# Two-layer encoder on one core: a reworked opening, and one step moved ahead of a store in the tail

## The chip, the core and the metric

The kernel runs on one core of a Trainium2 chip. The core has five instruction queues: TensorE (PE in the profile; its weight loads are listed as PEld), VectorE (DVE), ScalarE (ACT), GpSimd (POOL) and SyncE (SP). SyncE here does nothing but issue transfers; ScalarE and GpSimd issue some too. Each queue runs in its own order, and an instruction waits for semaphores that other queues or transfers set. The metric is the device time of one execution in microseconds (us), lower is better.

## The reference

Input and output are 512 tokens by 1024 features in float32. Two layers run one after the other. Each normalizes x, projects it by a 1024 x 3072 matrix, runs eight heads of stick-breaking attention and four pairs of differential attention, projects back and adds to x; then comes a dense block with a squared ReLU. A last normalization ends it.

```python
for l in range(DEPTH):
    h = rmsnorm(x, attn_norm[l])
    proj = jnp.einsum('bsd,de->bse', h, w_in[l])
    ...
    x = x + jnp.einsum('bse,ed->bsd', mixed, w_o[l])
    h = rmsnorm(x, mlp_norm[l])
    u = jnp.square(jax.nn.relu(jnp.einsum('bsd,df->bsf', h, w_ff1[l])))
    x = x + jnp.einsum('bsf,fd->bsd', u, w_ff2[l])
return rmsnorm(x, final_norm)
```

`rmsnorm(x, g)` is x times the inverse root of the mean of its squares over the features, times g.

## The kernel before

**Layout.** x lies transposed in SBUF: eight chunks (numbered 0 to 7) of 128 features by 512 tokens. A float32 product is made of three TensorE products. Each operand is split into a rounded high part (`hi`) and the rest (`lo`), and hi*hi, hi*lo and lo*hi are added in PSUM. ScalarE makes the high part, VectorE the low part by a subtraction that needs the high part. So for every chunk of x and every block of weights there is a step on ScalarE, then one on VectorE, then products on TensorE.

**Opening.** The first layer's normalization factor is applied after the projection, so TensorE can begin as soon as the first chunk has landed and has been scaled by its gains (`make_h`, line 249). The first two weight units, `raws[0]` and `raws[1]` (called unit 0 and unit 1 here; tiles `whi0`, `wlo0`, `whi1`, `wlo1`), feed two PSUM banks `p00` and `p01`. Both need all eight chunks. Each unit has eight blocks of 128 columns, block c for chunk c. The tile `begin` holds the gains and block 0 of unit 0; it comes over ScalarE's transfer queue, and so do blocks 1 to 3 of unit 0. The chunks of x and the rest of both units come over SyncE's queue in the order of lines 205 to 209.

**Warm-up.** Eight products of zeros (lines 222 and 223) run on TensorE ahead of the data. They read the zero part of the tile `edge`, which GpSimd sets (line 217) behind the set-up of the identity matrix (line 214).

**Order.** A scheduler places the instructions of each queue, guided by the order of the code and by the pairs given to `behind(a, b)`, which puts a after b on one engine. The order is fixed at build time. Each transfer from SyncE or ScalarE takes the next of eight semaphores in turn, and the ninth waits until the first has landed, and so on.

**Tail.** The last product form ("22") of the last group finishes the output, one row of 128 tokens after another: rows 0, 1, 2 and 3, each in two halves of 512 features. For a row, `square` on ScalarE adds up the squares of both halves, `root` adds them on VectorE (line 1161) and takes the power -1/2 on GpSimd (line 1163), and `store` multiplies one half on VectorE and the other on ScalarE and issues the transfers. Row 3 goes through `last_row` and `store_last` in quarters. Two lists, `first` for VectorE and `squares` for ScalarE, are chained by `in_order` (line 1286), so their order is that of lines 1250 to 1255.

Of the kernel before, what the change touches and what calls it, by code (L numbers as in the profile page):

```python
# [9 lines left out]
F32 = mybir.dt.float32  # L10
F32R = mybir.dt.float32r
BF16 = mybir.dt.bfloat16
AF = mybir.ActivationFunctionType
# [4 lines left out]
P = 128  # L18
S = 512
# [146 lines left out]
def trunk(ctx, tc, opened, xT, w, w2, w1, gfin, lamv, cos, sin, out):  # L166
    nc = tc.nc
# [10 lines left out]
    def bank(tag, name):  # L178
        if tag == "any":
            tag = ("mm", "s", "s", "mm", "s")[turn[0] % 5]  # L180
            turn[0] += 1
        ring[0] += tag == "s"
        return ps.tile([P, 512], F32, tag=tag, name=name, bufs=banks[tag])
# [17 lines left out]
    lam_ex = cp.tile([P, L, 2], F32, tag="lamex", name="lam_ex")  # L201
    raws = [wraw.tile([P, 1024], F32, tag="raw", name=f"raw{i}") for i in range(2)]
    nc.scalar.dma_start(begin, opened)
    nc.scalar.dma_start(raws[0][:, P : 4 * P], w[0][:, P : 4 * P])
    for c in range(KC):
        nc.sync.dma_start(x[:, c, :], xT[c])
        if c % 2 == 0:
            for i in range(c < 4, 2):
                nc.sync.dma_start(raws[i][:, c * P : (c + 2) * P], w[i][:, c * P : (c + 2) * P])
    W.raw = dict(enumerate(raws))  # L210
    W.loaded = 2
    W.load(3)

    make_identity(nc, ident)
    mhalf = cp.tile([P, 4], F32, tag="mhalf", name="mhalf")
    nc.vector.memset(mhalf, -0.5)
    nc.gpsimd.memset(edge[:, 0:384], 0.0)
    prime = cp.tile([P, 1], F32, tag="prime", name="prime")
    nc.scalar.activation(prime, mhalf[:, 0:1], AF.Exp)
    zeros = edge.bitcast(BF16)  # L220
    pw = bank("t", "warm")
    for _ in range(WARM):
        nc.tensor.matmul(pw, zeros[:, 0:128], zeros[:, 128:640], start=True, stop=True)

    def gcol(which, l, c):
        i = {"attn": l * 8, "mlp": 16 + l * 8, "final": 32, "sub": 40 + l}[which] + c
# [19 lines left out]
            out=lo, in0=src, scalar=-1.0, in1=hi.bitcast(F32), op0=ALU.mult, op1=ALU.subtract)  # L246
        return a

    def make_h(c, g):
        a = nc.scalar.activation(h_hi[:, c, :], x[:, c, :], AF.Copy, scale=g)  # L250
        return a, nc.vector.scalar_tensor_tensor(
            out=h_lo[:, c, :], in0=x[:, c, :], scalar=g, in1=h_hi[:, c, :].bitcast(F32),
            op0=ALU.mult, op1=ALU.subtract)

    def add_sq(c, first, sqt, eng=nc.gpsimd):
# [80 lines left out]
    for l in range(L):  # L336
        with ExitStack() as actx:
# [22 lines left out]
            if l == 0:  # L360
                W.eager = True
                W.split_part(0, 0, P)
                W.eager = False
                opened = make_h(0, gcol("attn", 0, 0))
                behind(opened[1], W.last[1])
                W.split_part(1, 0, 2 * P)
                for a, b in zip(W.last, opened):
                    behind(a, b)
                ahead = W.last
                W.split_part(0, P, 2 * P)  # L370
                for a, b in zip(W.last, ahead):
                    behind(a, b)
                for c in range(1, KC):
                    if c % 2 == 0:
                        for i in range(2):
                            W.split_part(i, c * P, (c + 2) * P)
                            if (c, i) == (2, 0):
                                for a, b in zip(W.last, opened):
                                    behind(a, b)
                    opened = make_h(c, gcol("attn", 0, c))  # L380
                    if c == 1:
                        for a, b in zip(opened, W.last):
                            behind(a, b)
                W.split = 2
            else:
                pts, halfway, opened = opened_by.pop()
# [399 lines left out]
            def dense(pts):  # L786
                if l == 0:
                    us = [W.next("x"), W.next("x")]
                    pts = [bank("mm", f"p{l}{i}") for i in range(2)]
                    for i, m in ((0, 0), (0, 2), (1, 0), (0, 1), (1, 1), (1, 2)):  # L790
                        a, b = wpair(us[i], 0), hpair(0)
                        nc.tensor.matmul(pts[i], a[m == 2], b[m == 1], start=m == 0, stop=False)
                    yield 6 * 0.216
                    for i, m in ((0, 0), (1, 0), (0, 2), (1, 2), (0, 1), (1, 1)):
                        a, b = wpair(us[i], 1), hpair(1)
                        nc.tensor.matmul(pts[i], a[m == 2], b[m == 1], start=False, stop=False)
                    yield 6 * 0.216
                    turns = [(c, i) for c in range(2, 5) for i in range(2)] + [(c, i) for i in range(2) for c in (5, 6, 7)]
                    for c, i in turns:
                        three(pts[i], wpair(us[i], c), hpair(c), False, c == KC - 1)  # L800
                        yield 3 * 0.216
                step, b = 2 * KC, int(ORDER[0][1])
                held = [(pts[0], "d", b, "q"), (pts[1], "d", b, "k")]
                def walk(name, kind, b, which):
                    if kind in "wu":
                        for _ in all_values() if kind == "w" else values_of(b):
                            yield None
                    else:
# [50 lines left out]
        with ExitStack() as fctx:  # L859
# [331 lines left out]
            for g in range(GROUPS):  # L1191
# [24 lines left out]
                for form in FORMS2:  # L1216
# [20 lines left out]
                    for n, (c, i, r, part) in enumerate(work):  # L1237
# [11 lines left out]
                              opens and n == mine[0] and part < 2, n == mine[-1], not opens)  # L1249
                        if tail and last and n == 3:  # L1250
                            squares += [square(0, 0), seed, square(1, 0)]
                            first += [weighed[2], turned[1], came[1], root(0), weighed[3], store(0, 0, False)]
                            squares.append(store(0, 1, True))
                            first += [root(1), *gather(total, to, (0,)), store(1, 0, False)]
                            squares += [store(1, 1, True), square(2, 1)]
                        if end and not last and form == "22" and n % 2:
                            h = back(n // 2)
# [122 lines left out]
```

## Time and profile before

| What | us |
|---|---|
| median of 3 runs (lowest, highest) | 1124.26 (1123.91, 1124.55) |
| the profiled execution's own time | 1124.27 |
| its span, first to last instruction | 1122.5 |
| around the span in that execution | 1.77 |
| TensorE busy in the span | 1114.8 |
| VectorE, ScalarE, GpSimd busy | 903.4, 682.7, 153.6 |

In the timeline a row gives the start, the length, the engine (with a q for its instruction queue, where transfers are issued), the line, the operation, the tiles written and read, the shapes, and how many were merged; behind it in brackets stands how long the engine had been idle and what ended that. Matmuls overlap, so their rate is read from starts, not from lengths. The rows on transfers give the time from issue until the data had landed.

### The profile page before, as it was taken

Reading aid. Unit: us, or ns where it says so; the run is one execution under the profiler, and the core shown is the slowest. Engines: PE = TensorE matmul, PEld = TensorE weight load, DVE = VectorE, ACT = ScalarE, POOL = GpSimd, SP = SyncE. Lnnn points to the kernel's source line nnn. Section 1 sums busy time; section 2 is a strip of 40 time slices with the busy share of each in tenths; the row PEclk is TensorE's granted clock in tenths of the full one; section 3 lists DMA queues with packets and bytes.
Section 4 is the critical chain, followed back from the end, with each engine's and each line's share of the span. In section 5 each row is a group of like instructions: output and inputs, shape, how many; then the busy total and the mean of one; then the engine's idle time right before and its main releaser. Section 6 shows DMA issues by size and latency. Waiting matters only on the chain.

```text
span 1122.5 us, 17199 instructions
## 1 busy us (share of the span) xinstructions
PE 1114.8 (99%) x6377; PEld 978.2 (87%) x6377; DVE 903.4 (80%) x1309; ACT 682.7 (61%) x1107; POOL 153.6 (14%) x233
## 2 busy tenths in 40 slices
PE   9999999999999999999999999999999999999997
PEld 7889889888899899899878898988888998998986
DVE  7788788798668779779877887887787787797787
ACT  6446666667558457467344566665774584674665
POOL 1001344101011001001000014430011010010010
PEclk9999999999999999999999999999999999999999
DMA  7466343268687678658325654512676786787462
GB/s 249 137 191 184 112 133 114 73 220 232 172 217 169 182 200 185 189 134 211 109 75 148 197 146 130 168 59 76 209 175 183 202 189 175 184 185 206 113 132 94
DMA packets 61043, 181.25 MB, mean 161 GB/s; under 512 B 7456, under 2 KB 8736, under 8 KB 60960
## 3 DMA queue, kind: packets, MB, share of 16 engines
q1 hardware_dynamic: 50160, 141.84, 40.0%
q0 software_dynamic: 10368, 37.75, 19.2%
q8 instruction: 50, 0.82, 0.3%
q10 hardware_dynamic: 432, 0.56, 0.1%
q14 instruction: 33, 0.27, 0.1%
HBM read 150.77 MB, written 4.19 MB: 138 GB/s over the span
## 4 chain that ended last, share of the span: by engine, by line
PE 98%; DVE 1%; issue 0%; POOL 0%; ACT 0%; POOLq 0%; DVEq 0%
PE X L300 9%; PE X L302 9%; PE X L301 9%; PE V L300 4%; PE V L302 4%; PE V L301 4%; PE wo L300 3%; PE wo L301 3%; PE wo L302 3%; PE f L300 3%; PE f L302 3%; PE f L301 3%; PE Y L300 2%; PE Y L302 2%; PE Y L301 2%; PE W L302 1%
## 5 line engine op out<-in xcount | busy, mean ns | idle before, releaser
L117 ACT ACTIVATE whi<-q 128x1024 fp32r<-128x1024 f32 x96 | 101.7, 1059 | 108.5 <-PE X L302 38.1
L133 DVE TENSOR_TENSOR wlo<-q,whi 128x1024 fp32r<-128x1024 f32 x96 | 117.1, 1222 | 46.5 <-ACT whi L117 46.3
L133 DVE TENSOR_TENSOR wlo<-raw,whi 128x1024 fp32r<-128x1024 f32 (+1 forms) x82 | 97.2, 1191 | 11.0 <-ACT whi L117 11.0
L117 ACT ACTIVATE whi<-raw 128x1024 fp32r<-128x1024 f32 (+1 forms) x82 | 80.8, 993 | 37.6 <-issue 8.9
L300 PE MATMUL X<-whi,Ah 128*128 128x512 f32 x248 | 97.7, 394 | 0.0
L301 PE MATMUL X<-wlo,Ah 128*128 128x512 f32 x248 | 96.8, 390 | 0.0
L302 PE MATMUL X<-whi,Al 128*128 128x512 f32 x248 | 96.7, 390 | 0.0
L133 DVE TENSOR_TENSOR wlo<-waves,whi 128x1024 fp32r<-128x1024 f32 x40 | 48.9, 1221 | 16.5 <-ACT whi L117 16.4
L117 ACT ACTIVATE whi<-waves 128x1024 fp32r<-128x1024 f32 x40 | 42.2, 1055 | 29.7 <-PE X L302 20.5
L300 PEld LDWEIGHTS X<-whi,Ah 128*128 128x128 f32 x248 | 46.6, 188 | 12.0 <-DVE y L1104 1.9
L302 PEld LDWEIGHTS X<-whi,Al 128*128 128x128 f32 x248 | 46.6, 188 | 9.9
L302 PE MATMUL X<-hxh,wlo 128*128 128x256 f32 x192 | 54.4, 283 | 0.0
L302 PE MATMUL X<-h_hi,wlo 128*128 128x256 f32 x192 | 54.4, 283 | 0.0
L301 PE MATMUL X<-hxl,whi 128*128 128x256 f32 x192 | 54.4, 283 | 0.0
L301 PE MATMUL X<-h_lo,whi 128*128 128x256 f32 x192 | 54.4, 283 | 0.0
L300 PE MATMUL X<-hxh,whi 128*128 128x256 f32 x192 | 54.4, 283 | 0.0
L301 PEld LDWEIGHTS X<-wlo,Ah 128*128 128x128 f32 x248 | 46.6, 188 | 8.9
L300 PE MATMUL X<-h_hi,whi 128*128 128x256 f32 x192 | 54.4, 283 | 0.0
L300 PE MATMUL f<-h_hi,whi 128*128 128x512 f32 x128 | 50.4, 394 | 0.0
L302 PE MATMUL f<-h_hi,wlo 128*128 128x512 f32 x128 | 49.9, 390 | 0.0
L301 PE MATMUL f<-h_lo,whi 128*128 128x512 f32 x128 | 49.9, 389 | 0.0
L240 DVE TENSOR_TENSOR Al<-x,Ah 128x512 fp32r<-128x512 f32 (+1 forms) x60 | 46.5, 792 | 3.8 <-ACT Ah L239 3.5
(712 smaller groups left out, 3702.6 us busy)
## 6 DMA issues: line engine op xcount, KB each, us to landing
raw<-in_w SPq DMA_DIRECT2D x78, 512.0 KB, 3.6
q<-in_w SPq DMA_DIRECT2D x48, 512.0 KB, 4.6
q<-in_w POOLq DMA_DIRECT2D x48, 512.0 KB, 7.6
waves<-in_w SPq DMA_DIRECT2D x28, 512.0 KB, 4.5
first_a<-in_w SPq DMA_DIRECT2D x12, 512.0 KB, 4.7
first_b<-in_w SPq DMA_DIRECT2D x12, 512.0 KB, 5.2
first_c<-in_w SPq DMA_DIRECT2D x12, 512.0 KB, 4.3
first_b<-in_w POOLq DMA_DIRECT2D x12, 512.0 KB, 6.7
```

What stands on the lines that cost most here:

```text
L117: return self.nc.scalar.activation(o, src, AF.Copy)
L133: self.last = h, nc.vector.tensor_tensor(out=lo[:, a:b], in0=raw[:, a:b], in1=hi[:, a:b].bitcast(F32), op=ALU.subtract)
L240: nc.vector.tensor_tensor(out=lo, in0=src, in1=hi.bitcast(F32), op=ALU.subtract)
L300: nc.tensor.matmul(pt, ah, bh, start=first, stop=False, skip_group_check=goes_on),
L301: nc.tensor.matmul(pt, ah, bl, start=False, stop=False, skip_group_check=goes_on),
L302: nc.tensor.matmul(pt, al, bh, start=False, stop=last, skip_group_check=goes_on))
```

## The change

Opening:
- The warm-up products read a single zero (the low half of the float32 value -0.5 in the tile `mhalf`), broadcast over both operands, so they wait for VectorE's small write of `mhalf` and no longer for GpSimd's `edge`.
- Chunk 0 of x is loaded in two halves of 256 tokens, scaled in halves, and its first two products with unit 0 (high by high, high by low) are issued in halves too.
- Block 0 of unit 1 is loaded alone over ScalarE's queue, between `begin` and blocks 1 to 3 of unit 0; on SyncE's queue only block 1 of that unit is left at that place. The splits of blocks 0 and 1 are made one block at a time in a given order.

Tail: `root(1)`, the second row's sum and power, is put ahead of VectorE's store of the first row.

```diff
     nc.scalar.dma_start(begin, opened)
+    nc.scalar.dma_start(raws[1][:, 0:P], w[1][:, 0:P])
     nc.scalar.dma_start(raws[0][:, P : 4 * P], w[0][:, P : 4 * P])
     for c in range(KC):
-        nc.sync.dma_start(x[:, c, :], xT[c])
+        for t in ([slice(0, 256), slice(256, S)] if c == 0 else [slice(0, S)]):
+            nc.sync.dma_start(x[:, c, t], xT[c][:, t])
         if c % 2 == 0:
             for i in range(c < 4, 2):
-                nc.sync.dma_start(raws[i][:, c * P : (c + 2) * P], w[i][:, c * P : (c + 2) * P])
+                a = max(c, 1) * P
+                nc.sync.dma_start(raws[i][:, a : (c + 2) * P], w[i][:, a : (c + 2) * P])
...
-    make_identity(nc, ident)
     mhalf = cp.tile([P, 4], F32, tag="mhalf", name="mhalf")
     nc.vector.memset(mhalf, -0.5)
+    make_identity(nc, ident)
     nc.gpsimd.memset(edge[:, 0:384], 0.0)
...
+    nought = mhalf.bitcast(BF16)[:, 0:1]
     for _ in range(WARM):
-        nc.tensor.matmul(pw, zeros[:, 0:128], zeros[:, 128:640], start=True, stop=True)
+        nc.tensor.matmul(pw, nought.to_broadcast([P, P]), nought.to_broadcast([P, S]), start=True, stop=True)
...
-                opened = make_h(0, gcol("attn", 0, 0))
-                behind(opened[1], W.last[1])
-                W.split_part(1, 0, 2 * P)
-                for a, b in zip(W.last, opened):
-                    behind(a, b)
-                ahead = W.last
-                W.split_part(0, P, 2 * P)
-                for a, b in zip(W.last, ahead):
-                    behind(a, b)
+                halves = [slice(0, 256), slice(256, S)]
+                for t in halves:
+                    ahead, opened = W.last, make_h(0, gcol("attn", 0, 0), t)
+                    behind(opened[1], ahead[1])
+                    W.last = opened
+                for i, c in ((1, 0), (0, 1), (1, 1)):
+                    ahead = W.last
+                    W.split_part(i, c * P, c * P + P)
+                    for a, b in zip(W.last, ahead):
+                        behind(a, b)
...
-                        nc.tensor.matmul(pts[i], a[m == 2], b[m == 1], start=m == 0, stop=False)
+                        for t in halves if (i, m) in ((0, 0), (0, 2)) else [slice(0, S)]:
+                            nc.tensor.matmul(pts[i][:, t], a[m == 2], b[m == 1][:, t], start=m == 0 and not t.start, stop=False)
...
-                            first += [weighed[2], turned[1], came[1], root(0), weighed[3], store(0, 0, False)]
+                            first += [weighed[2], turned[1], came[1], root(0), weighed[3], root(1), store(0, 0, False)]
                             squares.append(store(0, 1, True))
-                            first += [root(1), *gather(total, to, (0,)), store(1, 0, False)]
+                            first += [*gather(total, to, (0,)), store(1, 0, False)]
```

On ScalarE, this is the order of the opening before, from the scaling of chunk 0 on (`h_hi` is a scaled chunk's high part, `whi0` and `whi1` are those of units 0 and 1; the fourth and sixth rows are chunks 1 and 2, the eighth is chunks 3 and 4):

```order
L250 ACTIVATE h_hi_72<-x_71,begin_70 128x512
L117 ACTIVATE whi1_151<-raw1_80 128x256
L117 ACTIVATE whi0_145<-raw0_79 128x128
L250 ACTIVATE h_hi_72<-x_71,begin_70 128x512
L117 ACTIVATE whi0_145<-raw0_79 128x256
L250 ACTIVATE h_hi_72<-x_71,begin_70 128x512
L117 ACTIVATE whi1_151<-raw1_80 128x256
L250 ACTIVATE h_hi_72<-x_71,begin_70 128x512 x2
```

And this is ScalarE's order there after the change:

```order
L254 ACTIVATE h_hi_72<-x_71,begin_70 128x256 x2
L117 ACTIVATE whi1_155<-raw1_80 128x128
L117 ACTIVATE whi0_147<-raw0_79 128x128
L117 ACTIVATE whi1_155<-raw1_80 128x128
L254 ACTIVATE h_hi_72<-x_71,begin_70 128x512
L117 ACTIVATE whi0_147<-raw0_79 128x256
L117 ACTIVATE whi1_155<-raw1_80 128x256
L254 ACTIVATE h_hi_72<-x_71,begin_70 128x512 x3
```

Beside the halves and single blocks, one more thing moved: the split of blocks 2 and 3 of unit 1 (the 128x256 row of `whi1`) stood behind the scaling of chunk 2 and now stands ahead of it, and VectorE's low parts are ordered in the same way.

On SyncE, these are the first transfers before, with the semaphore that the issue waits for:

```order
L206 DMA x_71<-in_xT 128x512
L209 DMA raw1_80<-in_w 128x256
L206 DMA x_71<-in_xT 128x512 x2
L209 DMA raw1_80<-in_w 128x256
L206 DMA x_71<-in_xT 128x512
L206 DMA x_71<-in_xT 128x512 [waits DMAHW0_49]
```

And these after (semaphore 0 is that of `begin`, the first transfer of ScalarE's queue, in both):

```order
L208 DMA x_71<-in_xT 128x256 x2
L212 DMA raw1_80<-in_w 128x128
L208 DMA x_71<-in_xT 128x512 x2
L212 DMA raw1_80<-in_w 128x256 [waits DMAHW0_49]
L208 DMA x_71<-in_xT 128x512 [waits DMAHW1_49]
L208 DMA x_71<-in_xT 128x512 [waits DMAHW2_49]
```

With two more transfers ahead, the one of blocks 2 and 3 of unit 1 is the ninth and is issued only when `begin` has landed; before it was the seventh and was issued without a wait.

On VectorE, this is the tail before, from `root(0)` on (`fin` holds the sums and powers, `y00` the first halves of rows 0 and 1, `Z11` the bank of row 2):

```order
L1161 TENSOR_SCALAR fin_123<-fin_123 128x1
L1168 TENSOR_TENSOR y01_1_8184<-y01_1_8184,x_71 128x512
L1176 SCALAR_TENSOR_TENSOR y00_1_8182<-y00_1_8182,fin_123,x_71 128x512
L1161 TENSOR_SCALAR fin_123<-fin_123 128x1
L1104 SCALAR_TENSOR_TENSOR y11_1_8185<-Z11_11029,r2_122,y11_1_8185 128x512
```

And this is the same stretch after:

```order
L1167 TENSOR_SCALAR fin_125<-fin_125 128x1
L1174 TENSOR_TENSOR y01_1_8192<-y01_1_8192,x_71 128x512
L1167 TENSOR_SCALAR fin_125<-fin_125 128x1
L1182 SCALAR_TENSOR_TENSOR y00_1_8190<-y00_1_8190,fin_125,x_71 128x512
L1110 SCALAR_TENSOR_TENSOR y11_1_8193<-Z11_11037,r2_124,y11_1_8193 128x512
```

The second sum stands ahead of the first row's store; nothing else in VectorE's tail moved, and ScalarE's and GpSimd's orders there are as before.

More of the change, by code (lines that the diff above doesn't have):

```diff
@@ L247, in split_less, with make_h @@
         return a
-    def make_h(c, g):
-        a = nc.scalar.activation(h_hi[:, c, :], x[:, c, :], AF.Copy, scale=g)
+    def make_h(c, g, t=slice(0, S)):
+        a = nc.scalar.activation(h_hi[:, c, t], x[:, c, t], AF.Copy, scale=g)
         return a, nc.vector.scalar_tensor_tensor(
-            out=h_lo[:, c, :], in0=x[:, c, :], scalar=g, in1=h_hi[:, c, :].bitcast(F32),
+            out=h_lo[:, c, t], in0=x[:, c, t], scalar=g, in1=h_hi[:, c, t].bitcast(F32),
             op0=ALU.mult, op1=ALU.subtract)
```

## The prediction

> **What bounds the kernel.** I read the page's totals and its chain first, then the timeline of the first 10 us and of the last 12, because the change touches only these two stretches.
>
> ```profile
> span 1122.5 us, 17199 instructions
> ...
> PE 1114.8 (99%) x6377; PEld 978.2 (87%) x6377; DVE 903.4 (80%) x1309; ACT 682.7 (61%) x1107; POOL 153.6 (14%) x233
> ...
> PE 98%; DVE 1%; issue 0%; POOL 0%; ACT 0%; POOLq 0%; DVEq 0%
> ```
>
> The chain that ended last is 98% TensorE. So what TensorE gains in the opening stays until the end, unless data hold it later. The few us at both ends are where other engines are on the chain. These rows of the timeline are the opening:
>
> ```profile
> 0.82 0.06 DVE L216 MEMSET mhalf<- 128x4 f32 x1 [0.82 <-PEq L1369]
> 0.88 0.42 POOL L217 MEMSET edge<- 128x384 f32 x1
> 1.19 0.45 ACTq L204 DMA_DIRECT2D raw<-in_w  x1
> 1.36 3.59 PE L223 MATMUL warm<-edge 128*128 128x512 bf16 x8 [1.36 <-POOL edge L217]
> 1.66 0.90 SPq L206 DMA_DIRECT2D x<-in_xT  x2
> 1.67 1.28 ACT L219 ACT_TABLE_LOAD   x1 [1.67 <-PEq L1369]
> 2.60 0.43 SPq L209 DMA_DIRECT2D raw<-in_w  x1
> 2.96 0.20 ACT L219 ACTIVATE prime<-mhalf 128x1 f32<-128x1 f32 x1
> 4.16 0.72 ACT L250 ACTIVATE h_hi<-x,begin 128x512 fp32r<-128x512 f32 x1 [0.99 <-DMA begin<-in_opened]
> 4.93 0.80 PE L792 MATMUL p<-h_hi,whi 128*128 128x512 f32 x1
> 5.95 0.63 PE L792 MATMUL p<-h_hi,whi 128*128 128x512 f32 x1
> 6.38 0.97 PE L792 MATMUL p<-h_lo,whi 128*128 128x512 f32 x2
> 6.76 0.72 ACT L250 ACTIVATE h_hi<-x,begin 128x512 fp32r<-128x512 f32 x1 [0.18 <-DMA x<-in_xT]
> 7.39 0.40 ACT L117 ACTIVATE whi<-raw 128x256 fp32r<-128x256 f32 x1
> 7.42 0.63 PE L796 MATMUL p<-h_hi,whi 128*128 128x512 f32 x2
> 7.51 0.75 DVE L251 SCALAR_TENSOR_TENSOR h_lo<-x,begin,h_hi 128x512 fp32r<-128x512 f32 x1
> 8.79 0.39 PE L300 MATMUL p<-h_hi,whi 128*128 128x512 f32 x1
> 9.02 0.39 PE L301 MATMUL p<-h_lo,whi 128*128 128x512 f32 x1
> 9.02 0.71 ACT L117 ACTIVATE whi<-raw 128x256 fp32r<-128x256 f32 x2
> ```
>
> The first product starts at 4.93. Starts lie 0.43 us apart at first (5.95, 6.38) and 0.23 apart later (8.79, 9.02): TensorE's clock doubles shortly before 7.2, some 5.7 us after the warm-up began. From 4.93 on TensorE has no gap. Chunk 2 begins at 8.79 (line 300) and needs the low part of its x at 9.02; that row of VectorE (7.51, 0.75 long) ends at 8.26, 0.76 earlier. That slack limits what a faster start can bring.
>
> **The opening, part by part.** *Warm-up.* It waited for GpSimd until 1.30; `mhalf` is done at 0.88. With the 0.06 us from the end of that write to 1.36, the warm-up starts at 0.94, 0.42 earlier, and its eight products of 0.43 end near 4.38. The broadcast read has no row; I take it as no slower, since one row of 512 elements still passes per column. GpSimd's identity matrix is needed far later, so the swap of lines costs nothing.
>
> *First scaling.* ScalarE waited for `begin`, by the row at 4.16; this is its row among the transfers, the last figure being us from issue to landing:
>
> ```profile
> begin<-in_opened ACTq DMA_DIRECT2D x1, 96.0 KB, 3.4
> ```
>
> Smaller rows of x beside `begin` can only bring it forward; it lands at 4.15 at the latest. On ScalarE one issue more (0.45) stands ahead of the table load: 1.67 + 0.45 + 1.28, then 0.20 for `prime`, so ScalarE is free near 3.63. A scaling of half the width has this row:
>
> ```profile
> L1005 ACT ACTIVATE x<-x,begin x8: 492/495/512, 241.9 to 810.0; 128x256 f32<-128x256 f32 x8
> ```
>
> The first half is ready between 4.13 and 4.65, and the first product starts between 4.40 (behind the warm-up) and 4.70, that is 0.23 to 0.53 before 4.93. The four half products pass no more columns than two whole ones. ScalarE's and VectorE's extra pieces (two halves of 0.49 for one step of 0.72, one split more) lie ahead of chunk 1, for whose data they wait anyway. The single block of unit 1 follows `begin` on its queue and is used third, 0.86 after that start, so I cost it at nothing; its cover is those first products. Were it late, the wait would come out of the lead that TensorE has on the data (below).
>
> *The catch.* ScalarE now splits blocks 2 and 3 of unit 1 ahead of scaling chunk 2. That split needs a transfer which landed behind chunk 2's:
>
> ```profile
> x<-in_xT SPq DMA_DIRECT2D x1, 256.0 KB, 4.6
> ...
> raw<-in_w SPq DMA_DIRECT2D x1, 128.0 KB, 4.5
> ```
>
> Chunk 2, the second in the row at 1.66, was issued at 2.13 and landed at 6.73, 0.03 ahead of its scaling at 6.76. The weights, issued at 2.60, landed at 7.08. As many bytes stand ahead of them as before, so at best 7.08 holds again. Then the split starts at 7.10, the next step 0.31 later (in the row at 9.02 two such splits, 0.40 each, take 0.71), chunk 2's high part runs 7.41 to 8.13, its low part 8.16 to 8.91, and the product that needs it starts at 8.95. It is now the third of chunk 2, not the second; the third was at 9.25. So data allow a gain of 0.30. TensorE alone could gain more: with the clock step 0.42 earlier too, near 6.75, 5.5 products of 0.43 from 4.40 on and the other 6.5 of the first two chunks at 0.23 end at 8.24 instead of 8.79, a gain of 0.55.
>
> The other end: that transfer now waits for `begin` before it is issued, 4.15 at the latest, and with the 3.4 that `begin` itself took it lands at 7.55. Then 0.30 becomes a loss of 0.17. Since the 4.5 is nearly all queueing behind the same bytes, I take 0.1 of delay: a gain of 0.2, ends +0.55 and -0.17. Behind chunk 2 the same lateness of some 0.3 on ScalarE runs into slack: its splits at 9.02 are for chunks 4 and 5, used two chunks (2.7 us) after 8.79.
>
> *The clock.* By the Trainium skill, page TensorE: Matmul & The Clock Gate, Part 1, the clock is judged in free-running windows of 3.4 us and rises after a window that was busy. The 5.7 us seen here fit that, as one cut window and one whole one. By the rule, the latest rise after a start at 0.94 would be at 7.8; then chunk 2 starts near 8.7 and the opening gains 0.1 instead of 0.2, and the sum below would be 1123.9.
>
> **The tail, step by step.**
>
> ```profile
> 1112.38 0.19 ACT L1127 ACTIVATION_READ_ACCUMULATOR x<-y 128x1 f32 x1
> 1112.66 0.75 DVE L1176 SCALAR_TENSOR_TENSOR y<-y,fin,x 128x512 f32<-128x512 f32 x1 [0.47 <-POOL fin L1163]
> 1113.33 0.21 DVE L1161 TENSOR_SCALAR fin<-fin 128x1 f32<-128x1 f32 x1
> 1113.45 0.74 DVE L1104 SCALAR_TENSOR_TENSOR y<-Z,r,y 128x512 f32<-128x512 f32 x1
> 1113.62 0.55 POOL L1163 TENSOR_TENSOR fin<-fin,mhalf 128x1 f32<-128x1 f32 x1 [0.99 <-DVE fin L1161]
> 1114.20 0.72 ACT L1174 ACTIVATE y<-y,fin 128x512 f32<-128x512 f32 x1 [0.82 <-POOL fin L1163]
> 1114.83 0.62 ACT L1127 ACTIVATE x<-y 128x512 f32<-128x512 f32 x1
> 1114.87 0.48 DVE L1132 SCALAR_TENSOR_TENSOR y<-Z,r,y 128x256 f32<-128x256 f32 x1
> 1115.57 0.21 DVE L1161 TENSOR_SCALAR fin<-fin 128x1 f32<-128x1 f32 x1 [0.22 <-ACT x L1127]
> 1116.28 0.47 ACT L1139 ACTIVATE x<-half,r 128x256 f32<-128x256 f32 x1 [0.33 <-PE half L302]
> 1116.44 0.75 DVE L1176 SCALAR_TENSOR_TENSOR y<-y,fin,x 128x512 f32<-128x512 f32 x1 [0.24 <-POOL fin L1163]
> 1116.65 0.19 ACT L1139 ACTIVATION_READ_ACCUMULATOR x<-half,r 128x1 f32 x1
> 1117.11 0.15 DVE L1144 TENSOR_TENSOR fin<-fin 128x1 f32<-128x1 f32 x1
> 1118.67 0.35 ACTq L1178 DMA_DIRECT2D out_xT<-y  x1
> ```
>
> The second row's squares are summed at 1112.57 (1112.38 + 0.19), while VectorE idles until 1112.66 and GpSimd for 0.99 until 1113.62. Moved, `root(1)` runs at 1112.60. It takes 0.12 of VectorE (1113.33 to 1113.45), so the first row's store slips by 0.06 to 1112.72, and its transfer with it; nothing waits for that one. GpSimd's power starts 0.29 behind the sum, at 1112.89, and ends at 1113.44 instead of 1114.17. ScalarE's store of row 1 moves from 1114.20 to 1113.47, and the square behind it from 1114.83 to 1114.15, where VectorE's step of 1113.45 (now 1113.39, 0.74 long) releases it. Its sum is complete 0.72 later, at 1114.87. VectorE's chain is 0.1 ahead by then (1114.87 becomes 1114.78, held by the product it reads), and `root(2)` can run at 1115.26 instead of 1115.57. Row 2's store follows at 1116.13 instead of 1116.44 and frees VectorE at 1116.80.
>
> What is late next is TensorE itself: ScalarE's square at 1116.28 waits for the last products, and its sum ends at 1116.84. So the last addition moves from 1117.11 to 1116.87: 0.24. Everything behind it, down to the last issue at 1118.67, hangs on that addition. The ends: 0.27 (ScalarE's 1116.84 exactly) and 0, if a store or square stays where it is. I take 0.24.
>
> **Sum.** The profiled execution took 1124.27, equal to the median of 1124.26 within 0.01. 1124.27 - 0.20 - 0.24 = 1123.83, so 1123.8. That is 0.04%: a change is called faster or slower here only beyond 0.2% (2.25 us), which is about what a measurement of this kernel can tell from no change.
>
> **Rivals.**
> - *The clock starts over (slower).* The warm-up now ends at 4.38. If the data come at 4.70, TensorE idles 0.3 us, where it idled 0.15 before. If that gap made the 5.7 us count anew from 4.4, the clock would rise at 10.1 instead of 6.7. Products at half rate for 3.4 us cost 1.7: 1125.5. It decides from the point at which a gap that short counts as idle. Against it: 0.15 did not. Being slower by 0.2% would need a cold clock until about 12.
> - *The opening does not do what it says.* Issued behind `begin`, the weights land near 7.5, chunk 2 is late, and the earlier warm-up is eaten: 1124.27 + 0.17 - 0.24 = 1124.2. For it speaks the new wait; against it the full queue ahead.
> - *Data come sooner too.* With smaller first transfers everything up to chunk 2 lands 0.3 earlier and TensorE's own 0.55 is the gain: 1124.27 - 0.55 - 0.27 = 1123.5 (rounded). The unchanged bytes speak against it.
>
> **How the numbers follow.** My forecast 0.55, the eaten opening 0.22, sooner data 0.12, the restarted clock 0.07, something else 0.04. All four cases lie within 0.2%. The runs before spread over 0.6 us, so the range is 1123.5 less 0.6 to the eaten opening's 1124.2 plus 0.6, and 0.3 more towards the restarted clock, whose 1125.5 it leaves out: 1122.9 to 1125.1. Faster by over 0.2% gets 0.02, slower 0.03, the same 0.95.
>
> **What the profile after would show.** Warm-up from 0.94, first product at 4.4 to 4.7, the rate doubled before 7.2, chunk 2's low part at its product near 8.95 with TensorE waiting there, `root(1)` near 1112.6 less what the opening gave, and the last addition 0.24 nearer to TensorE's last product, with the same 1.56 us from it to the last issue. I am wrong if the blocks of unit 1 land later than 7.4, if the rate doubles after 8, or if the last addition does not follow the third row's store.

## The result, and the profile after

| | before | after |
|---|---|---|
| median of 21 runs | 1124.30 us | 1125.48 us |
| profiled execution | 1124.27 us | 1126.34 us |
| its span | 1122.5 us | 1124.5 us |

The median rose by 1.2 us, and the ratio, which goes by the means, is 1.0013 with a 95% interval of 1.0008 to 1.0019. That is a loss of a tenth of a per cent where a gain of 0.4 us was forecast, and it lies outside the range of 1122.9 to 1125.1. One of the 21 runs of after took 2250.33 us and tells nothing of the kernel. The profiled execution of after lies 0.86 above its median, so its numbers describe that execution, and are used only with their place in the program.

The page of after, its totals and its chain:

```profile
span 1124.5 us, 17211 instructions
...
PE 1116.3 (99%) x6379; PEld 977.8 (87%) x6379; DVE 903.5 (80%) x1311; ACT 683.2 (61%) x1109; POOL 153.9 (14%) x233
...
PE 95%; DVE 2%; DMA 2%; issue 1%; ACT 0%; POOL 0%; POOLq 0%; DVEq 0%; SPq 0%
```

TensorE had 98% of the chain and has 95%. DMA, which was not on it, now has 2%. The timeline of the opening shows where (start, duration, and in brackets the idle time before the row with what ended it):

```profile
0.94 3.60 PE L227 MATMUL warm<-mhalf 128*128 128x512 bf16 x8 [0.94 <-DVE mhalf L218]
...
1.66 0.43 SPq L212 DMA_DIRECT2D raw<-in_w  x1
1.67 0.45 ACTq L205 DMA_DIRECT2D raw<-in_w  x1
...
4.13 0.98 PE L798 MATMUL p<-h_hi,whi 128*128 128x256 f32 x2
...
5.76 1.05 PE L798 MATMUL p<-h_lo,whi 128*128 128x512 f32 x2
6.50 0.51 ACT L117 ACTIVATE whi<-raw 128x128 fp32r<-128x128 f32 x2 [1.83 <-DMA raw<-in_w]
6.62 0.51 PE L798 MATMUL p<-h_hi,wlo 128*128 128x512 f32 x1
...
7.16 0.72 ACT L254 ACTIVATE h_hi<-x,begin 128x512 fp32r<-128x512 f32 x1
...
7.93 0.73 PE L802 MATMUL p<-h_hi,whi 128*128 128x512 f32 x2 [0.80 <-ACT h_hi L254]
8.49 0.62 PE L802 MATMUL p<-h_hi,wlo 128*128 128x512 f32 x2
...
8.96 0.63 PE L802 MATMUL p<-h_lo,whi 128*128 128x512 f32 x2
...
9.43 0.63 PE L304 MATMUL p<-h_hi,whi 128*128 128x512 f32 x2
...
14.74 0.72 ACT L254 ACTIVATE h_hi<-x,begin 128x512 fp32r<-128x512 f32 x1 [1.78 <-DMA x<-in_xT]
...
15.51 0.73 PE L304 MATMUL p<-h_hi,whi 128*128 128x512 f32 x2 [0.18 <-ACT h_hi L254]
...
18.48 0.62 PE L304 MATMUL p0w<-mdh,h_hi 128*128 128x512 f32 x2
```

The start does what the change says: the warm-up begins at 0.94, the first product at 4.13 instead of 4.93. Then ScalarE stands still for 1.83 us, because unit 0's blocks 1 to 3 have not come. It splits block 1 of unit 0 at 6.50 and scales chunk 1 only at 7.16, and TensorE waits 0.80 us for that. Chunk 2 begins at 9.43, where it began at 8.79. Chunk 7 is late as well (ScalarE idle 1.78), and `p0w`, the first products behind the opening, start at 18.48. The same row of before:

```profile
16.95 0.84 PE L300 MATMUL p0w<-mdh,h_hi 128*128 128x512 f32 x3
```

So the opening costs 1.53 us in this execution: 0.64 stands at chunk 2's start, the rest is added by 18.48, on the way to which ScalarE's longest wait is that for chunk 7. That second part is not shown to be the change's: in tail_only below, whose opening is that of before, ScalarE idles 1.67 us for chunk 7 as well. The transfers issued in the first 2 us of after, with KB and the us from issue to landing:

```profile
x<-in_xT SPq DMA_DIRECT2D x2, 128.0 KB, 2.7
raw<-in_w ACTq DMA_DIRECT2D x1, 192.0 KB, 4.8
begin<-in_opened ACTq DMA_DIRECT2D x1, 96.0 KB, 2.8
raw<-in_w ACTq DMA_DIRECT2D x1, 64.0 KB, 2.9
raw<-in_w SPq DMA_DIRECT2D x1, 64.0 KB, 4.6
```

The single block of unit 1 (64 KB on ScalarE's queue) is not late: 2.9 us from 1.19. The one behind it, unit 0's blocks 1 to 3, took 4.8 from 1.67 and landed at 6.48; before, it was issued at 1.19 and landed at 4.89. SyncE's transfer of 1.66, a mere 64 KB, took 4.6. What the DMA engines moved between 3.5 and 5.0 us (the last figures are their busy share and GB/s), first of before:

```profile
3.50:5.00 1.50, 1.50 (x5) 0.34 (x3) 0.65 (x5) 0.84 (x2) 0.00 (x0) 1.00 1.12 346
```

and of after:

```profile
3.50:5.00 1.50, 1.50 (x6) 0.88 (x5) 1.43 (x7) 1.18 (x4) 0.00 (x0) 1.00 0.89 198
```

The engines are still occupied, but bring 198 GB/s instead of 346.

The tail of after:

```profile
1114.78 0.22 DVE L1167 TENSOR_SCALAR fin<-fin 128x1 f32<-128x1 f32 x1
...
1117.64 0.20 DVE L1167 TENSOR_SCALAR fin<-fin 128x1 f32<-128x1 f32 x1
...
1118.35 0.28 PE L306 MATMUL half<-whi,Al 128*128 128x256 f32 x1
...
1118.49 0.75 DVE L1182 SCALAR_TENSOR_TENSOR y<-y,fin,x 128x512 f32<-128x512 f32 x1
...
1119.33 0.16 DVE L1150 TENSOR_TENSOR fin<-fin 128x1 f32<-128x1 f32 x1
...
1120.90 0.35 ACTq L1184 DMA_DIRECT2D out_xT<-y  x1
```

TensorE's last product starts here at 1118.35. In before it starts at

```profile
1115.90 0.28 PE L302 MATMUL half<-whi,Al 128*128 128x256 f32 x1
```

From that product to the last addition it was 1.21 us (to 1117.11) and is 0.98 (to 1119.33). From there to the last issue it was 1.56 and is 1.57. So the tail gives 0.23, as forecast. The last product is 2.45 later than in before, and `p0w` was 1.53 later. The other 0.92 arose in between: with the products of both kernels paired in order, 0.44 of it comes between 21 and 28 us, where TensorE waits for VectorE at

```profile
24.38 0.63 PE L275 MATMUL rs_a<-edge,norms 128*128 128x128 f32 x4 [0.27 <-DVE lam_pr L330]
```

and 0.41 between 99 and 165 us, where swapped and alone_sync below lose 0.36 and 0.33 too. Whether late transfers are behind these steps is not shown.

### The profile page after: what moved, and what is told of

It is laid out like the page before. It is cut to its first block, busy times and chain, and to the rows that moved or that the text cites. A ratio compares the mean times of both kernels' runs of the same rounds, so it can differ in the third digit from the quotient of the medians.

```text
span 1124.5 us, 17211 instructions
## 1 busy us (share of the span) xinstructions
PE 1116.3 (99%) x6379; PEld 977.8 (87%) x6379; DVE 903.5 (80%) x1311; ACT 683.2 (61%) x1109; POOL 153.9 (14%) x233
## 4 chain that ended last, share of the span: by engine, by line
PE 95%; DVE 2%; DMA 2%; issue 1%; ACT 0%; POOL 0%; POOLq 0%; DVEq 0%; SPq 0%
PE X L304 9%; PE X L305 9%; PE X L306 9%; PE V L304 4%; PE V L305 4%; PE V L306 4%; PE wo L304 3%; PE wo L305 3%; PE wo L306 3%; PE f L306 3%; PE f L304 3%; PE f L305 3%; PE Y L304 2%; PE Y L305 2%; PE Y L306 2%; PE W L305 1%
## 5 line engine op out<-in xcount | busy, mean ns | idle before, releaser
L133 DVE TENSOR_TENSOR wlo<-raw,whi 128x1024 fp32r<-128x1024 f32 (+2 forms) x83 | 97.3, 1180 | 12.4 <-ACT whi L117 12.4
L117 ACT ACTIVATE whi<-raw 128x1024 fp32r<-128x1024 f32 (+2 forms) x83 | 81.0, 984 | 38.9 <-issue 8.9
```

The costliest lines, as they stand in the source:

```text
L117: return self.nc.scalar.activation(o, src, AF.Copy)
L133: self.last = h, nc.vector.tensor_tensor(out=lo[:, a:b], in0=raw[:, a:b], in1=hi[:, a:b].bitcast(F32), op=ALU.subtract)
```

## The experiments

Each kernel ran 11 times, and the runs of before beside it 33 times (medians 1123.93, 1124.15, 1124.06 and 1124.28 in the four groups). The intervals are about 0.09% to either side, 1 us, so single differences under that stay open. Each kernel has one profile, of one of its executions.

### The four parts, one at a time

Each has one part of the change on the kernel before.

tail_only:

```diff
-  first += [weighed[2], turned[1], came[1], root(0), weighed[3], store(0, 0, False)]
+  first += [weighed[2], turned[1], came[1], root(0), weighed[3], root(1), store(0, 0, False)]
```

> The kernel before with nothing but the second row's sum and power ahead of the first row's store. In the profile after, TensorE's last product is 2.45 us later than before and the end 2.03 us later, so the tail gave 0.42 there. Theory: the tail is a plain gain of 0.2 to 0.4 us (1123.9 to 1124.1 against 1124.3). Rival: in the profile after the gain came from the late opening, and alone it is within 0.1 us.

Measured 1123.69, 0.24 below its before, 0.9997 (0.9988 to 1.0006). The time alone can't confirm 0.24; its profile can:

```profile
1115.52 0.21 DVE L1163 TENSOR_SCALAR fin<-fin 128x1 f32<-128x1 f32 x1
...
1116.13 0.28 PE L302 MATMUL half<-whi,Al 128*128 128x256 f32 x1
...
1117.10 0.16 DVE L1146 TENSOR_TENSOR fin<-fin 128x1 f32<-128x1 f32 x1
```

The last addition follows the last product's start by 0.97 instead of 1.21.

warm_only:

```diff
+    mhalf = cp.tile([P, 4], F32, tag="mhalf", name="mhalf")
+    nc.vector.memset(mhalf, -0.5)
     make_identity(nc, ident)
-        nc.tensor.matmul(pw, zeros[:, 0:128], zeros[:, 128:640], start=True, stop=True)
+        nc.tensor.matmul(pw, nought.to_broadcast([P, P]), nought.to_broadcast([P, S]), start=True, stop=True)
```

> The kernel before with nothing but the broadcast warm-up. Theory (the loss is late transfers of the weight pieces): the warm-up starts at 0.94 instead of 1.36, the first product still waits for the first scaling near 4.9, the clock doubles up to 0.4 us earlier, so 0.0 to 0.3 us are gained. Rival (a clock that starts over after a gap): the warm-up ends at 4.4, TensorE idles 0.5 us until 4.9, which is more than after the whole change; then the rate doubles near 10 and 1 to 1.7 us are lost.

Measured 1124.04, 1.0003 (0.9994 to 1.0012): no difference. In its profile TensorE idles 0.72 us ahead of the first product, at 5.15, and the products from 5.49 on start 0.23 apart: that gap did not bring the slow clock.

x_only:

```diff
-        nc.sync.dma_start(x[:, c, :], xT[c])
+        for t in ([slice(0, 256), slice(256, S)] if c == 0 else [slice(0, S)]):
+            nc.sync.dma_start(x[:, c, t], xT[c][:, t])
```

> The kernel before with nothing but chunk 0 loaded, scaled and first multiplied in halves. Theory: the first scaling starts near 3.6 but TensorE still waits for its warm-up until 4.8; chunk 1 lands near 5.6; within 0.2 us of before. Rival (the halves hold the transfers back): chunk 1 lands near 7 and about 1 us is lost.

Measured 1123.96, 1.0001 (0.9992 to 1.0010): no difference.

alone_only:

```diff
     nc.scalar.dma_start(begin, opened)
+    nc.scalar.dma_start(raws[1][:, 0:P], w[1][:, 0:P])
     nc.scalar.dma_start(raws[0][:, P : 4 * P], w[0][:, P : 4 * P])
...
-                W.split_part(1, 0, 2 * P)
+                for i, c in ((1, 0), (0, 1), (1, 1)):
```

> The kernel before with nothing but the second unit's first block alone on ScalarE's queue and the splits block by block. Theory: the two pieces with 512 bytes a row and the later weights of unit 0 behind them hold back all transfers; chunk 1 lands near 7 us instead of 5.5 and 0.9 to 1.5 us are lost (1125.2 to 1125.8). Rival (the halves of chunk 0 hold the transfers back): chunk 1 lands near 5.6 and the loss is under 0.3 us, all of it from the split that now stands ahead of scaling chunk 2.

Measured 1124.94, 1.0009 (1.0000 to 1.0018): 1.0 us slower. Its interval just touches 1, and this part alone is nearly the loss of the whole. Its transfer of unit 0's blocks 1 to 3:

```profile
raw<-in_w ACTq DMA_DIRECT2D x1, 192.0 KB, 5.1
```

It landed at 6.75, as late as in after.

### Is it the order of the splits, or the transfer?

order_c2 puts the split of unit 1's blocks 2 and 3 back behind the scaling of chunk 2:

```diff
-                    opened = make_h(c, gcol("attn", 0, c))
+                    ahead, opened = W.last, make_h(c, gcol("attn", 0, c))
+                    if c == 2:
+                        for a, b in zip(ahead, opened):
+                            behind(a, b)
```

> The whole change, with ScalarE's and VectorE's split of blocks 2 and 3 of unit 1 put back behind the scaling of chunk 2. Theory A (the moved split is the loss, 0.9 to 1.2 us against before): the time comes back to 1123.6 to 1124.1. Theory B (the queue: with one more transfer ahead of them on ScalarE's queue, blocks 1 to 3 of unit 0 land near 6.5 us and chunk 1's scaling stands behind them): at most 0.3 us come back, 1124.9 to 1125.4.

split_as_before splits blocks 0 and 1 in pairs again:

```diff
-                for i, c in ((1, 0), (0, 1), (1, 1)):
+                for i, p, q in ((1, 0, 2), (0, 1, 2)):
                     ahead = W.last
-                    W.split_part(i, c * P, c * P + P)
+                    W.split_part(i, p * P, q * P)
```

> The whole change with its transfers, but the splits of blocks 0 and 1 of unit 1 in one piece as before; ScalarE's order at chunk 2 is then as before too. Theory A: 1123.6 to 1124.1, like the run with the order put back. Theory B: blocks 1 to 3 of unit 0 still land near 6.5, the loss stays: 1124.9 to 1125.5.

alone_sync loads the single block on SyncE's queue, so that ScalarE's has two transfers:

```diff
-    nc.scalar.dma_start(raws[1][:, 0:P], w[1][:, 0:P])
...
+                if c == 0:
+                    nc.sync.dma_start(raws[i][:, 0:P], w[i][:, 0:P])
```

> The whole change, but block 0 of unit 1 comes over SyncE's queue ahead of block 1, so ScalarE's queue holds two transfers as before; ScalarE's order at chunk 2 is as before. Theories A and B both: blocks 1 to 3 of unit 0 land near 5 us and the loss goes, 1123.5 to 1124.0. If small pieces as such hold the transfers back (theory C), the loss stays near 1125.2 here, where two transfers of 64 KB remain.

not_alone is the whole change without the single block, in transfers and splits:

```diff
-    nc.scalar.dma_start(raws[1][:, 0:P], w[1][:, 0:P])
...
-                a = max(c, 1) * P
-                nc.sync.dma_start(raws[i][:, a : (c + 2) * P], w[i][:, a : (c + 2) * P])
+                nc.sync.dma_start(raws[i][:, c * P : (c + 2) * P], w[i][:, c * P : (c + 2) * P])
...
-                for i, c in ((1, 0), (0, 1), (1, 1)):
+                for i, p, q in ((1, 0, 2), (0, 1, 2)):
```

> The whole change without the single block: warm-up, chunk 0 in halves and the tail stay. All theories: the loss goes with the single block. If the parts add up, this is before (0) + tail (-0.24) + warm-up (+0.1) + halves (0) = 1124.1 at before's 1124.3; if the earlier warm-up and the earlier first half only pay together, as the prediction reckoned, 0.2 to 0.3 us less.

Measured: order_c2 1125.59, 1.0012 (1.0004 to 1.0021); split_as_before 1126.46, 1.0018 (1.0009 to 1.0026); alone_sync 1124.64, 1.0002 (0.9993 to 1.0011); not_alone 1123.76, 0.9995 (0.9986 to 1.0004). The loss stays with either order of splits, so the order is not its cause. When the third transfer leaves ScalarE's queue it is gone in not_alone; in alone_sync 0.5 is left, against an expected end of the loss, with an interval that holds both 0 and 1.2 us. order_c2 and split_as_before are slower than the 1125.4 and 1125.5 that theory B allowed. The transfers of not_alone:

```profile
raw<-in_w ACTq DMA_DIRECT2D x1, 192.0 KB, 3.3
raw<-in_w SPq DMA_DIRECT2D x1, 128.0 KB, 3.2
```

Unit 0's blocks land at 4.53, and its timeline has no long wait:

```profile
4.09 1.03 PE L796 MATMUL p<-h_hi,whi 128*128 128x256 f32 x2
...
4.87 0.62 ACT L117 ACTIVATE whi<-raw 128x256 fp32r<-128x256 f32 x2 [0.18 <-DMA raw<-in_w]
...
5.86 0.72 ACT L252 ACTIVATE h_hi<-x,begin 128x512 fp32r<-128x512 f32 x1 [0.37 <-DMA x<-in_xT]
...
6.64 0.74 PE L800 MATMUL p<-h_hi,whi 128*128 128x512 f32 x2
```

### What about the third transfer?

swapped exchanges the second and the third on ScalarE's queue:

```diff
-    nc.scalar.dma_start(raws[1][:, 0:P], w[1][:, 0:P])
     nc.scalar.dma_start(raws[0][:, P : 4 * P], w[0][:, P : 4 * P])
+    nc.scalar.dma_start(raws[1][:, 0:P], w[1][:, 0:P])
```

> The whole change, with the second and third transfer of ScalarE's queue swapped: blocks 1 to 3 of unit 0 second, the single block of unit 1 third. Bytes, row sizes and the number of transfers are those of the changed kernel. Theory Q (whatever stands third on ScalarE's queue is late, with SyncE's transfer issued at the same moment): blocks 1 to 3 of unit 0 land near 4.9 as before, the single block near 6.5 and chunk 1 near 7.1; the time stays at 1125 or above. Theory R (the pieces with rows of 512 bytes are what slows the transfers behind them): blocks 1 to 3 of unit 0 land near 4.9 and so does chunk 1, near 5.6, since the single block has less behind it: 1124.0 or below.

pair_scalar has no rows of 512 bytes (splits as in not_alone):

```diff
-    nc.scalar.dma_start(raws[1][:, 0:P], w[1][:, 0:P])
+    nc.scalar.dma_start(raws[1][:, 0 : 2 * P], w[1][:, 0 : 2 * P])
```

> The whole change, but blocks 0 and 1 of unit 1 are one transfer again and stand second on ScalarE's queue, with blocks 1 to 3 of unit 0 third; no rows of 512 bytes are left, SyncE issues one transfer fewer. Theory Q: blocks 1 to 3 of unit 0 land near 6.5, chunk 1 near 7, and the time is 1125 or above. Theory R: they land below 5.2, chunk 1 below 6.2, and the time is that of the change without the single block, 1123.8, or 0.1 to 0.3 less, since SyncE issues chunk 1 some 0.45 earlier.

issue_late places the third issue behind the first activation:

```diff
-    nc.scalar.dma_start(raws[0][:, P : 4 * P], w[0][:, P : 4 * P])
...
     nc.scalar.activation(prime, mhalf[:, 0:1], AF.Exp)
+    nc.scalar.dma_start(raws[0][:, P : 4 * P], w[0][:, P : 4 * P])
```

> The whole change, but ScalarE issues its third transfer (blocks 1 to 3 of unit 0) only behind the table load and its first activation, near 3.2, not at 1.67 beside SyncE's issue. Theory C (two issues at the same moment, 1.66, disturb each other): unit 1's block 1, issued by SyncE at 1.66, lands near 4.9 and chunk 1 below 6.2, as where ScalarE issues two; the late one lands near 6.5. Theory Q: the third transfer itself holds the others up whenever it comes: chunk 1 lands near 7 as in the changed kernel. The time is near 1125 by both, as unit 0's blocks are late by both.

warm_tail is warm-up and tail alone (the edits of warm_only and tail_only):

> Warm-up and tail of the change alone; x of chunk 0 whole and loads as before. If the halves of x give nothing by themselves, as measured, this is as fast as the change without the single block: 1123.5 to 1123.9. If the halves were what let that version start sooner, this one stays at the sum of its parts, 1124.0 to 1124.2.

Measured: swapped 1124.59, 1.0005 (0.9996 to 1.0013); pair_scalar 1126.41, 1.0020 (1.0011 to 1.0029); issue_late 1126.21, 1.0019 (1.0010 to 1.0027); warm_tail 1123.98, 1.0000 (0.9991 to 1.0009).

pair_scalar is, with split_as_before, the slowest of all, without any rows of 512 bytes, so theory R falls. Its late transfers, the first SyncE's, of chunk 1:

```profile
x<-in_xT SPq DMA_DIRECT2D x1, 256.0 KB, 5.7
raw<-in_w ACTq DMA_DIRECT2D x1, 192.0 KB, 5.9
```

and what they do to its timeline:

```profile
5.01 0.40 PE L798 MATMUL p<-h_hi,whi 128*128 128x512 f32 x1
5.24 0.63 PE L798 MATMUL p<-h_lo,whi 128*128 128x512 f32 x2
...
7.59 0.31 ACT L117 ACTIVATE whi<-raw 128x128 fp32r<-128x128 f32 x1 [2.84 <-DMA raw<-in_w]
...
8.56 0.80 PE L802 MATMUL p<-h_hi,whi 128*128 128x512 f32 x1 [2.46 <-ACT h_hi L254]
```

In this execution, 1126.51 us, the loss is not the wait alone. Behind the gap of 2.46 the products from 9.16 to 11.29 start 0.43 apart again: the granted clock, the third figure from the end, was half.

```profile
9.50:11.30 1.80, 1.80 (x6) 1.33 (x5) 1.80 (x5) 1.80 (x5) 0.00 (x0) 0.50 0.95 293
```

In the profile of after it was not:

```profile
8.50:10.00 1.50, 1.50 (x7) 0.91 (x5) 1.50 (x5) 1.50 (x4) 0.00 (x0) 1.00 0.88 316
```

The profiles of split_as_before and of x1_behind below show the same half clock, behind gaps of 1.66 (and 0.30 soon after) and 2.18 us, each time for about 3.4 us, which at half rate costs up to 1.7 (estimate). Gaps of 1.30 in alone_only, 1.34 in order_c2 and 1.56 in issue_late did not bring it. The three executions with the half clock have a mean granted clock of 0.997, every other profiled one has 0.998 or more. Of the 20 usable executions of after, two have 0.997 (1127.01 and 1127.07 us), so these two probably lost this way too, which is not shown, as they have no profile; of the executions of before beside the experiments none has.

swapped lies between the theories: unit 0's blocks land at 4.44 as with two transfers, but the third lands at 5.83 and chunk 1 at 6.14, short of the 6.5 and 7.1 of theory Q:

```profile
raw<-in_w ACTq DMA_DIRECT2D x1, 192.0 KB, 3.3
...
raw<-in_w ACTq DMA_DIRECT2D x1, 64.0 KB, 4.2
```

issue_late did not test what it was made for: the instruction that issues a transfer did not wait for the activation ahead of it in the text, and was early still:

```profile
1.74 0.38 ACTq L222 DMA_DIRECT2D raw<-in_w  x1
```

Its profile is also that of its fastest execution, 1124.78 against a median of 1126.21. Whether the two issues at 1.66 disturb each other stays untested. warm_tail lies between its two expectations and doesn't decide between them.

### Third in its queue, or beside chunk 1?

In the late kernels unit 0's blocks are also read at the same time as chunk 1. Three kernels part the two.

x1_ahead: two transfers on ScalarE's queue, chunk 1 ahead of unit 1's pair on SyncE's:

```diff
+        if c == 1:
+            nc.sync.dma_start(raws[1][:, 0 : 2 * P], w[1][:, 0 : 2 * P])
-        if c % 2 == 0:
+        if c % 2 == 0 and c > 0:
```

> The change without the single block (two transfers on ScalarE's queue), but SyncE issues chunk 1 of x ahead of blocks 0 and 1 of unit 1, so that chunk 1 is read while unit 0's blocks 1 to 3 are. Theory Q (the third transfer on ScalarE's queue is the cause): unit 0's blocks land near 4.6 as with any two, chunk 1 near 5.5. Theory B (these two transfers together are slow): both land at 6.2 or later. Time: blocks 0 and 1 of unit 1 come near 6 instead of 4.85 by either, so TensorE waits about 1 us for them; 1124.0 to 1125.0 by Q, 1125.5 or more by B.

x1_behind: as pair_scalar, but unit 1's blocks 2 and 3 ahead of chunk 1:

```diff
+        if c == 0:
+            nc.sync.dma_start(raws[1][:, 2 * P : 4 * P], w[1][:, 2 * P : 4 * P])
-        if c % 2 == 0:
+        if c % 2 == 0 and c > 2:
```

> Three transfers on ScalarE's queue (opened, blocks 0 and 1 of unit 1, blocks 1 to 3 of unit 0), but SyncE issues blocks 2 and 3 of unit 1 at 1.66 and chunk 1 of x behind them. Theory Q: unit 0's blocks 1 to 3 land at 6.5 or later, as with three transfers before (7.57 in the nearest kernel). Theory B: they land below 5.3, since most of them is read beside other weights. The time by Q is 1125.5 to 1126.5, by B 1124.5 (chunk 1 some 0.4 late) or less.

third_unit1: as not_alone, with unit 1's blocks 2 and 3 third on ScalarE's queue:

```diff
     nc.scalar.dma_start(raws[0][:, P : 4 * P], w[0][:, P : 4 * P])
+    nc.scalar.dma_start(raws[1][:, 2 * P : 4 * P], w[1][:, 2 * P : 4 * P])
...
-        if c % 2 == 0:
+        if c % 2 == 0 and c != 2:
```

> The change without the single block, but blocks 2 and 3 of unit 1 are taken from SyncE's queue and stand third on ScalarE's, issued near 1.67; unit 0's blocks 1 to 3 stay second. Theory Q: the third lands at 6.5 or later, and SyncE's transfer of 1.66 (blocks 0 and 1 of unit 1) and chunk 1 behind it land 0.5 us or more later than the 4.85 and 5.84 of the kernel with two. Theory B: unit 0's blocks are through before chunk 1 begins, so nothing is late; the third lands near 5.5. The time is 1124.5 or above by Q, 1123.8 or below by B.

not_alone_again is not_alone once more, on another chip:

> The change without the single block, the same kernel as not_alone once more. If its gain is what the first comparison showed, it is 0.2 to 0.6 below before; if that was chance, it is within 0.1 of it.

Measured: x1_ahead 1124.57, 1.0003 (0.9994 to 1.0012); x1_behind 1125.72, 1.0015 (1.0006 to 1.0024); third_unit1 1125.40, 1.0014 (1.0005 to 1.0023); not_alone_again 1123.45, 0.9994 (0.9985 to 1.0003), 0.83 below its before where a real gain was put at 0.2 to 0.6.

With two transfers, chunk 1 and unit 0's blocks go together without harm (x1_ahead):

```profile
x<-in_xT SPq DMA_DIRECT2D x1, 256.0 KB, 4.0
raw<-in_w ACTq DMA_DIRECT2D x1, 192.0 KB, 3.8
```

With three they are late also beside other weights (x1_behind):

```profile
raw<-in_w ACTq DMA_DIRECT2D x1, 192.0 KB, 5.7
...
raw<-in_w SPq DMA_DIRECT2D x1, 128.0 KB, 5.6
```

So theory B falls. third_unit1 is between again: unit 0's blocks, second, land at 4.62, the third at 5.70 (4.0 from its issue), chunk 1 at 6.02. Its median is 1.1 us above before all the same. The profile cannot tell why: it is of the fastest of the eleven executions, 1123.89, in which TensorE's last product comes no later than in before, while seven took 1125.2 to 1127.6, two of them with the mean clock of 0.997. So a third transfer costs time here even where unit 0's blocks stand second, and late blocks of unit 0 are not shown to be its only price.

All profiles together, us:

| unit 0's blocks 1 to 3 on ScalarE's queue | profiles | they land | chunk 1 lands |
|---|---|---|---|
| second, nothing third (before, the kernels without a third, x1_ahead) | 9 | 4.44 to 5.24 | 5.36 to 6.31 |
| second, another transfer third (swapped, third_unit1) | 2 | 4.44, 4.62 | 6.14, 6.02 |
| third (after, alone_only, order_c2, split_as_before, pair_scalar, issue_late, x1_behind) | 7 | 6.38 to 7.57 | 6.57 to 7.89 |

What is shown: with a transfer of weights put ahead of unit 0's blocks on ScalarE's queue, these land 1.1 us or more behind the latest of the others, in each of the seven profiles with it and in none of the other eleven. In swapped the same three transfers in another order do not delay them. In all seven, third place also means an issue at 1.66 to 1.74 instead of 1.19, beside SyncE's of 1.66; no run separates the place from that moment. How the chip comes to it stays open. The low rate goes with it: between 3.5 and 5.0 us six of the seven move 145 to 198 GB/s and the eleven others 278 to 375. It is not all of it, since the seventh, alone_only, moved 334 in the same 1.5 us:

```profile
3.50:5.00 1.50, 1.48 (x5) 0.39 (x4) 0.69 (x5) 1.03 (x3) 0.00 (x0) 1.00 1.06 334
```

There the bytes came, but other ones than ScalarE waited for.

## Why the prediction was wrong

*First product: the direction right, the size beaten.* 4.40 to 4.70 was forecast, 4.13 came. `begin` landed at 3.55, 2.8 us after its issue; I had used only that it comes "at 4.15 at the latest". The warm-up started at 0.94 as worked out. Its row of eight ends only at 4.54 (0.94 + 3.60), but the first product did not wait for that end, as I had it do.

*The step that failed: "As many bytes stand ahead of them as before, so at best 7.08 holds again", and the single block that "I cost at nothing".* I followed the block that was taken out, and it was indeed in time. I did not cost what was pushed back by it. Unit 0's blocks 1 to 3 went from second to third place on ScalarE's queue, and of that I counted only one issue more (0.45) ahead of the table load; the landing of these blocks is in no term of the sum. They landed 1.6 us later (6.48 for 4.89), ScalarE idled 1.83, and chunk 1 was scaled at 7.16, with TensorE waiting 0.80 for it. Counting bytes did not tell when a transfer lands: SyncE's 64 KB of 1.66 took 4.6 us, and unit 1's blocks 2 and 3, issued at 3.56 when `begin` had landed, came at 8.16, where 7.08 was called the best and 7.4 the sign of being wrong. The term for the opening was -0.20, with ends of -0.55 and +0.17. The whole measured 1.18 over before; with the tail's 0.24 back, all that is not tail is +1.4. In the profile it is 1.53 by `p0w` and 2.45 by the last product.

*The catch: not reached.* I had chunk 2 wait for unit 1's blocks 2 and 3. TensorE was held by chunk 1 before that; ScalarE went from unit 0's blocks to those of unit 1 without a wait (two splits from 7.78 to 8.60, the blocks there at 8.16). And order_c2, which undoes this very order, was 1.4 us slower than before (1.0004 to 1.0021). The mechanism could still bind where nothing else is late; no run shows it to.

*The tail: right.* 0.24 forecast, 0.23 in the profile of after, 0.24 in that of tail_only. Row 2's root came 0.61 ahead of the last product's start in tail_only (1115.52 against 1116.13), 0.33 in before: 0.28 earlier, where 0.31 was worked out.

*The rivals.* "The opening does not do what it says" had the sign of the opening's term and a wait for weights of unit 1; the weights were unit 0's and the price 1.4, not 0.17. "The clock starts over" gave the time that came, 1125.5, by luck: in the profile of after TensorE has no gap at the first product, and the products from 8.49 to 9.43 start 0.23 us apart, so the clock was up before the 10.1 of that rival. Its mechanism does exist in these kernels, at another place: the clock fell back behind the wait for chunk 1 where that was long, in three profiles and by their mean clock probably in two of the 20 executions of after. "Data come sooner too" was right of `begin` (0.6 earlier) and of the first half of x, wrong of all that followed.

*Without the single block* the forecast is about what happens. not_alone is 0.39 and 0.83 us below its befores; 0.44 was the sum. Either interval still holds 1, so it is the version that lies furthest below its befores, not one shown to be faster than before.

## What to carry to other kernels

When a transfer is put ahead on a queue, cost the one that it pushes back first: find who waits for that one, and bound its lateness by the longest time to landing among its neighbours, not by the issue that is added. In before that was 4.7 us, and 1.67 + 4.7 gives 6.4 where 6.48 came; pair_scalar's 7.57 shows that more can come. Then look how long TensorE would stand: behind waits of 1.66 us and more three of these kernels ran at half rate. Bytes ahead do not tell when a transfer lands while the queues are filling. Before a first transfer is cut up to start a few tenths sooner, look at which second transfer the next idle row names.

## What was not expected of the hardware

*One more transfer on a queue cost far more than its issue.* The Trainium skill, page DMA: Bandwidth & Descriptors, section Issuing engines are not separate DMA queues, says that issuing from several engines saves only the issuing time, since all use the same DMA engines. By that, moving 64 KB from SyncE's queue to ScalarE's would be worth about the 0.45 us of an issue. Here the same 64 KB on SyncE's queue (alone_sync) leaves unit 0's blocks at 4.44, and on ScalarE's ahead of them they land at 6.48. By the Trainium skill, the same page, section Queues, rings and completion order, each DMA engine takes turns between the queues; 64 KB more ahead in the same queue, at half of the 346 GB/s that before moved, would be another 0.4 us (estimate). Measured were 2.0 against alone_sync and 1.6 against before, twice the two or more, and no run here separates what makes up the rest.

*When TensorE's clock doubles varies between runs.* From the same start, 0.94, pair_scalar's products are already 0.23 apart from 5.01 to 5.24, 4.1 us after it; in after they are still 0.43 apart from 5.76 to 6.62, 5.7 us after it. The prediction's sum took 5.7 us as fixed. The Trainium skill, page TensorE: Matmul & The Clock Gate, Part 1, has windows of 3.4 us that run free of the kernel; from that, a rise 3.4 to 6.8 us after the start is an estimate, and the rows agree. The 1.6 us between the two, at half rate, are worth up to 0.8 us where TensorE has its data (estimate), about as much as single runs of one kernel differ by here; that this is why they differ was not tried.
